# Sums of the second up projection's weights: from VectorE in the projections to adding DMAs in the attention, with two rings of places for the weights

## The chip, the cores and the metric

The kernel runs on one core of a Trainium2 chip. The core has a matrix engine (TensorE, PE in the profile, with its weight loads as PEld), VectorE (DVE), ScalarE (ACT), GpSimd (POOL), a queue engine for DMAs (SP) and 16 DMA engines that all queues share. The metric is the device time of one execution in microseconds (us); a profiled execution lists each instruction, what it waited for and how long.

## What is computed

One layer of a decoder with two parallel token mixers, for 512 positions and a model width of 2048, all in float32. What matters here:

```python
proj = h @ w_in                        # h = RMSNorm(x)
o_a = nsa_attention(q, kv ...) * silu(z_a)
o_b = spatial_gating(uv, ...) * silu(z_b)
merged = g_a * (o_a @ w_up_a) + g_b * (o_b @ w_up_b)
x = x + merged @ w_out
x = x + sigmoid(x @ w_ple_gate) * (p @ w_ple)
return rms_norm(x, final_g)
```

The second up projection is `o_b @ w_up_b`: a 512x1024 by a 1024x2048 product.

## The kernel before

**Precision.** Every float32 matrix is split into a high part (fp32r) and a low part, the rest; a product is three matmuls, high x high, high x low and low x high. ScalarE makes the high part of weights (`high`, line 147), VectorE the low part (`low`, line 153), and TensorE needs both.

**Seven products for eight.** Large products ("S" jobs) take 2x2 blocks by a scheme of Winograd's kind: sums and differences of blocks on both sides, seven products, and sums of the results. The blocks of a weight are b11, b12 (first half of the rows; left and right 512 columns), b21, b22 (second half). The kernel of before uses, for the products named 5, 6, 7 and 4: t5 = b12 - b11, t6 = b22 - t5, t7 = t6 - b11 (made as b22 - b12), t4 = b21 - t6. For most jobs `sum_to` makes them on VectorE (line 271) just before the product. For the two jobs of the second up projection (ub0 and ub1, 1024 columns each) they are made early and kept in DRAM, in `up_sums[i][p]`, and loaded as weights are. The activations of the products have sums of their own (`put_steps`; `ob_dram` holds the parts for ub).

**How the sums are made before.** `up_set(i, k)` (lines 1034 to 1058), for each of the two jobs and four row blocks, has steps: `load` (four 256 KB DMAs on POOL's queue from `w_up_b` into two places `ab` and `cd` of the ring, line 1046), an empty step, `first` and `second`, each with two 128x512 subtractions on VectorE (line 1041) and a 256 KB store behind each on POOL's queue (line 1042), and an empty step. The 40 steps lie in the list `slow`.

**The order of the work.** `gemm()` is a generator that writes out the matmuls of all jobs in order; it yields after every three matmuls, and `fill(n)` takes n such units. At each piece of weights ("sub") it splits the weights of the sub two ahead (`split_to`), which also issues loads on SP's queue where a place has come free (`load_next`), and calls `pop`. `pop` takes a step off `slow` at a rate of 0.85 per call, and steps off `background` at the rate `state["pops"]`. All engines work their own instructions in program order; a wait stops that engine's queue alone. So a DMA on POOL's queue starts when POOL comes to it and what it waits for is there, not when TensorE comes to that place in the program.

**Stages.** Norm and per-layer embedding (0 to about 46 us); the K/V projections: jobs kc, vc, k, then vs (256 columns) and vw (304 columns), until 198 us; beside them `h_chunk` makes the split sums of the activations, with 16 stores of 512 KB on POOL's queue through a tile of three places (h_stage). Then the attention (about 206 to 511 us), in which the jobs q1 to q7 and za0 to za7 (56 subs) are filled in between the attention's own matmuls; POOL has the folds (lines 1285 and 1287), the gating of the compressed branch (1333) and stores of the result (o_d, line 577). `evac_q` asserts that `slow` is empty. Then the jobs u, vn, zb and the merge gates, the first up projection (ua0, ua1), the second (ub0, ub1; about 1130 to 1214 us), the output projection and the end.

**Places of the weights.** `raw` is a tile of three places, 512 KB each; `b12` one of four, for a block that `sum_to` writes into; `add_load` notes the tag and which earlier load must be done with. For ub all loads take `raw`. The activations of ub come back from DRAM by `load_ob(0..6)` on POOL's queue, into places that products of ua1 must have left; `load_gate_b(cg)` loads 1 MB of merge gates for a group of 512 columns, also on POOL's queue, and `gates_a` puts the first gates' multiplications (line 809) into `background`. `final_up` (line 811) closes a product of ub: a multiply on VectorE (line 816) and an addition on POOL (line 817).

Of the kernel before, what the change touches and what calls it, by code (L numbers as in the profile page):

```python
# [13 lines left out]
F32 = mybir.dt.float32  # L14
# [3 lines left out]
ALU = mybir.AluOpType  # L18
# [3 lines left out]
P = 128  # L22
# [42 lines left out]
def kernel(ctx: ExitStack, tc: tile.TileContext, x, p, norm_g, w_in,  # L65
# [108 lines left out]
    def add_load(tag, src, n, cols):  # L174
        r = ring_loads[tag]
        before.append(r[-rings[tag]] if len(r) >= rings[tag] else None)
        r.append(len(loads))
        loads.append((tag, src, n, cols))
        last_sub.append(None)
        return len(loads) - 1  # L180
# [4 lines left out]
    def add_job(job):  # L185
        jobs.append(job)
        if job.kind == "S":
            half, c2 = job.kt // 2, job.c2
            ld = {}
            if job.sums:  # L190
                for p, j in products(job):
                    c, k = {"1": (job.c0, 0), "2": (job.c0, half), "3": (c2, half)}.get(p, (0, 0))
                    src = weights(job, k + 2 * j, 2, c) if p in "123" else job.sums[p][:, 2 * j:2 * j + 2]
                    ld[p, j] = add_load("raw", src, 2, job.cols)
                    last_sub[ld[p, j]] = len(subs)
                    subs.append((job, p, j, ld))
                return
            direct = job.order[0] == "1"
            groups = [[(tag, j) for j in range(half // 2) for tag in tags] for tags in
                      ((("b11",), ("b21",), ("b12",), ("b22",), ("b21'",)) if direct else (("b11", "b12"), ("b22",), ("b21",)))]  # L200
            if direct:
                groups[2].append(groups[1].pop())
            for group in groups:
                for tag, j in group:
                    c, k = (job.c0, c2)[tag[2] == "2"], half * (tag[1] == "2") + 2 * j
                    ld[tag, j] = add_load(tag if tag[1] == "1" else "raw", weights(job, k, 2, c), 2, job.cols)
            for p, j in products(job):
                if not direct:
                    ld["b21'", j] = ld["b21", j]
                last = {"7": ("b11",), "4": ("b12", "b21'"), "3": ("b22",)}.get(p, ())  # L210
                if direct and p == "2":
                    last = ("b21",)
                for tag in last:
                    last_sub[ld[tag, j]] = len(subs)
                subs.append((job, p, j, ld))
            return
        first = 0
        while first < job.kt:
            n = min(job.per_load, job.kt - first)
            li = add_load("raw", weights(job, first, n, job.c0), n, job.cols)  # L220
            for k in range(first, first + n, job.per_sub):
                last_sub[li] = len(subs)
                subs.append((job, k, min(job.per_sub, first + n - k), (li, first)))
            first += n
# [4 lines left out]
    def ring(i, dtype, n=2):  # L229

        return quad["ring"].tile([P, n, S], dtype, tag=f"b11{i}", name="b11")
# [107 lines left out]
    slow = deque()  # L339

    def pop():
        state["late"] += 0.85
        if state["late"] >= 1:
            state["late"] -= 1
            if slow:
                slow.popleft()()
        state["due"] += state["pops"]
        while state["due"] >= 1:
            state["due"] -= 1
            if background:  # L350
                background.popleft()()
# [99 lines left out]
    def finish(name):  # L451
        while name not in done:
            next(run)
        flush()
# [3 lines left out]
    def sub(o, x, y, op=ALU.subtract):  # L458
        x, y = (i.bitcast(F32) if i.dtype == F32R else i for i in (x, y))
        nc.vector.tensor_tensor(out=o, in0=x, in1=y, op=op)  # L460

    def add(o, x, y):
        sub(o, x, y, ALU.add)
# [90 lines left out]

    def evac_q(ft):
        def f(ps):
            assert not slow
            pair = ring((0, 3, 2)[ft % 3], F32R)
            for hh in range(2):
                h = 2 * ft + hh  # L560
                sc = 0.125 / SLOPE[h]
                q = pair[:, hh]
                a = slice(64 * hh, 64 * hh + 64)
                b = slice(64 - 64 * hh, 128 - 64 * hh)
                split(q[a], q[b], ps[a], sc, later=True)
                qs[h] = q
        return f
# [242 lines left out]
                                       op0=ALU.add, op1=ALU.mult)  # L810

    def final_up(i):
        def f(t, c, o, src):
            cg = 2 * i + c // 512
            g, m = (parts_of[n][cg][:, t] for n in "lh")
            nc.vector.scalar_tensor_tensor(out=g, in0=g, scalar=1.0, in1=src, op0=ALU.add, op1=ALU.mult)
            nc.gpsimd.tensor_tensor(out=m, in0=m, in1=g, op=ALU.add)
        return f

    for i in range(2):  # L820
# [210 lines left out]
        split_to(13)  # L1031
    ph_r = ExitStack()
    quad["ring"] = ph_r.enter_context(tc.tile_pool(name="ring", bufs=1))
    ab, cd = (ring(i, F32) for i in range(2))

    def up_set(i, k):

        a, b, c, d = ab[:, 0], ab[:, 1], cd[:, 0], cd[:, 1]

        def minus(o, x, y, p):  # L1040
            nc.vector.tensor_tensor(out=o, in0=x, in1=y, op=ALU.subtract)
            nc.gpsimd.dma_start(up_sums[i][p][:, k], o)

        def load():
            for o, f, col in ((a, k, 0), (b, k, 512), (c, k + 4, 512), (d, k + 4, 0)):
                nc.gpsimd.dma_start(o, w_up_b[f * P:f * P + P, 1024 * i + col:1024 * i + col + 512])

        def first():
            minus(b, b, a, "5")
            minus(c, c, b, "6")  # L1050

        def second():
            minus(a, c, a, "7")
            minus(d, d, c, "4")
        return [load, lambda: None, first, second, lambda: None]

    for i in range(2):
        for k in range(4):
            slow.extend(up_set(i, k))
    mid = ph_ab.enter_context(tc.tile_pool(name="mid", bufs=1))  # L1060
    vt = mid.tile([P, 2, TT, GROUPS, 2 * HD], F32R, name="vt")
    gates = mid.tile([P, TT, 48], F32, name="gates")
# [101 lines left out]
    state["pops"] = 2  # L1164


    ph_b = ph_ab.enter_context(ExitStack())
    att = ph_b.enter_context(tc.tile_pool(name="att", bufs=1))
    tmp_pool.update(p=att, n=1, tag="zt")
# [248 lines left out]
        nc.gpsimd.dma_start(wn[hf], sgu_w[4 * hf:4 * hf + 4].rearrange("g t s -> t g s"))  # L1418
    nc.gpsimd.dma_start(bn, sgu_b)
    finish("za7")  # L1420
    for _ in range(2):
        flush()
    ph_o.close()
# [2 lines left out]
    def new_s4(q, dtype=F32R):  # L1426
        t = s4p.tile([P, 4, S], dtype, tag=f"s4{q}", name=f"s4{q}")
        return t

    def put_steps(w, c, dst, scale):  # L1430

        def put(n, tags, places, sl=slice(0, 512)):

            def f():
                width = sl.stop - sl.start
                h = mix["pool"].tile([P, S], F32R, tag=tags[0], name="pt_" + tags[0], bufs=2 if tags[0] == "v" else 1)
                if len(tags) == 2:
                    l = mix["pool"].tile([P, S], F32R, tag=tags[1], name="pt_" + tags[1])
                else:
                    l = w[n].bitcast(F32R) if width == 512 else h[:, 256:]  # L1440
                high(h[:, :width], w[n][:, sl], scale)

                def rest():
                    low(h[:, :width], l[:, :width], w[n][:, sl], scale)
                    for j, i in enumerate(places):
                        for a, o in enumerate((h, l)):
                            nc.gpsimd.dma_start(dst[:, i, a, c], o[:, 256 * j:256 * j + 256])
                deferred.append(rest)
            return f

        def sums_13():
            f1, f2 = w["1"], w["2"]
            add(f2[:, hi_t], f2[:, hi_t], f1[:, hi_t])
            sub(f1[:, hi_t], f1[:, lo_t], f1[:, hi_t])

        def sums_24():
            f1, f2 = w["1"], w["2"]
            sub(f1[:, lo_t], f2[:, hi_t], f1[:, lo_t])
            sub(f2[:, lo_t], f2[:, lo_t], f1[:, lo_t])
        return put, sums_13, sums_24  # L1460

    def oa_chunk(c):
# [166 lines left out]

    def group_pair(c):  # L1630
        both = {}
        put, sums_13, sums_24 = put_steps(both, c, ob_dram, None)

        def sums_put():
            sums_24()
            put("1", ("g0",), (2, 4))()
        return (group(c, both) + group(c + 4, both) + [nothing, put("2", ("g0", "g1"), (5, 6)), nothing, nothing,
                put("1", ("v",), (0,), lo_t), sums_13, sums_put, nothing, put("2", ("g1",), (3, 1)), nothing])
# [65 lines left out]


    load_ob(5, new_s4(1))
    load_ob(6, new_x(F32R))
    gates_a((2, 3))
    for cg in range(2):
        load_gate_b(cg)  # L1710

    def turn_merged(i, banks, n):

# [240 lines left out]
```

## Time and profile before

| | us |
|---|---|
| median of 3 runs (1562.84 to 1565.43) | 1564.43 |
| the profiled execution | 1564.91 |
| its span | 1562.9 |
| VectorE's waits for loads of w_up_b at line 1041 | 16.6 |
| mean granted clock of TensorE | 0.994 |

The profile's page gives busy time by engine, DMA queues, the chain that ended last and the costliest groups. A row of a wait reads: engine, what it was about to write and its line, the engine or DMA waited for; then us in total, times, longest. A row of a timeline reads: start, length, engine, line, operation, output and inputs, sizes; in brackets the idle time ahead of it and who ended it. Matmuls overlap, so their start-to-start distance tells the rate.

### The profile page before, as it was taken

How to read it: one execution, taken by the hardware profiler on the slowest of the kernel's cores; microseconds unless marked ns; L12 is line 12 of the kernel's file. 1: busy time of each engine (PE TensorE's matmuls, PEld its weight loads, DVE VectorE, ACT ScalarE, POOL GpSimd, SP SyncE). 2: the span in 40 equal slices, each digit the busy share in tenths (PEclk: the TensorE clock that was granted, in tenths of full speed). 3: DMA queues.
4: the chain of work that ended last, by engine and by line, in shares of the span. 5: the costliest groups of instructions: out<-in, count | busy, mean ns of one | idle time of the engine just before them, and what ended most of it. 6: DMA issues, size and time to landing. Idle time of an engine off the chain costs nothing.

```text
span 1562.9 us, 20745 instructions
## 1 busy us (share of the span) xinstructions
PE 1535.5 (98%) x7390; PEld 1283.2 (82%) x7390; DVE 1244.4 (80%) x1933; ACT 805.8 (52%) x1369; POOL 317.8 (20%) x526
## 2 busy tenths in 40 slices
PE   9999899999999999999999999999999999999997
PEld 8888788888888888888888888888877888888886
DVE  6568747898887788978988787787878787878877
ACT  6433336676665555545455444555445343544455
POOL 1323300011022332301222121321123222000100
PEclk9999899999999999999999999999999999999999
DMA  8668852123223985836574746686676478454655
GB/s 320 208 189 267 274 157 68 48 61 102 55 81 122 320 247 175 272 97 208 168 286 108 241 140 221 225 276 242 238 276 221 141 232 266 149 197 167 188 200 191
DMA packets 174311, 298.62 MB, mean 191 GB/s; under 512 B 11752, under 2 KB 89216, under 8 KB 171008
## 3 DMA queue, kind: packets, MB, share of 16 engines
q1 hardware_dynamic: 117456, 157.96, 31.8%
q0 software_dynamic: 56608, 139.07, 26.9%
q8 instruction: 58, 0.95, 0.2%
q14 instruction: 45, 0.37, 0.1%
q10 hardware_dynamic: 144, 0.26, 0.0%
HBM read 227.52 MB, written 69.73 MB: 190 GB/s over the span
## 4 chain that ended last, share of the span: by engine, by line
PE 83%; DVE 5%; DMA 5%; issue 3%; ACT 2%; POOL 1%; DVEq 0%; POOLq 0%; ACTq 0%
PE ps_m L378 6%; PE ps_m L379 6%; PE ps_m L377 6%; PE ps_za L403 2%; PE ps_t L1248 2%; PE ps_za L404 2%; PE ps_za L405 2%; PE ps_wo L416 2%; PE ps_wo L417 2%; PE ps_wo L415 2%; PE ps_pg L378 2%; PE ps_wo L378 2%; PE ps_zb L378 2%; PE ps_vn L379 2%; PE ps_zb L379 2%
## 5 line engine op out<-in xcount | busy, mean ns | idle before, releaser
L147 ACT CAST hs<-b 128x1024 fp32r<-128x1024 f32 x196 | 205.9, 1053 | 226.2 <-PE ps_m L379 66.4
L153 DVE TENSOR_TENSOR ls<-b,hs 128x1024 fp32r<-128x1024 f32 x196 | 239.5, 1223 | 102.1 <-ACT hs L147 100.9
L147 ACT CAST hs<-raw 128x1024 fp32r<-128x1024 f32 x108 | 113.6, 1054 | 130.3 <-PE ps_m L379 28.2
L153 DVE TENSOR_TENSOR ls<-raw,hs 128x1024 fp32r<-128x1024 f32 x108 | 139.2, 1290 | 36.2 <-ACT hs L147 36.1
L153 DVE TENSOR_TENSOR lo<-raw,hi 128x512 fp32r<-128x512 f32 (+1 forms) x184 | 125.6, 688 | 43.6 <-issue 17.0
L147 ACT CAST hi<-raw 128x512 fp32r<-128x512 f32 (+1 forms) x184 | 108.3, 603 | 84.2 <-PE ps_wo L417 19.4
L377 PE MATMUL ps_m<-hs,act_h 128*128 128x512 f32 x256 | 100.5, 393 | 0.0
L378 PE MATMUL ps_m<-ls,act_h 128*128 128x512 f32 x256 | 100.0, 390 | 0.2 <-DVE ls L153 0.2
L379 PE MATMUL ps_m<-hs,act_l 128*128 128x512 f32 x256 | 99.7, 390 | 0.0
L271 DVE TENSOR_TENSOR b<-raw,b 128x1024 f32<-128x1024 f32 x80 | 97.4, 1218 | 1.4 <-DMA raw<-in_w_in_dram 1.0
L271 DVE TENSOR_TENSOR b<-b,b 128x1024 f32<-128x1024 f32 x80 | 97.4, 1218 | 0.0
L147 ACT CAST pth<-ps_t 128x512 fp32r<-128x512 f32 (+1 forms) x88 | 48.0, 545 | 65.8 <-PE ps_t L1248 65.5
L153 DVE TENSOR_TENSOR ptl<-ps_t,pth 128x512 fp32r<-128x512 f32 (+1 forms) x88 | 56.2, 638 | 21.0 <-ACT pth L147 20.0
L1209 ACT ACTIVATE prob<-prob,st 128x512 f32<-128x512 f32 (+3 forms) x128 | 70.7, 556 | 4.0 <-DVE st L1200 3.8
L1200 DVE CUSTOM_DVE_ANT_0 prob<-ps_s,b 128x512 f32<-128x512 f32 (+3 forms) x128 | 56.3, 486 | 10.0 <-PE ps_s L1197 9.7
L378 PEld LDWEIGHTS ps_m<-ls,act_h 128*128 128x128 f32 x256 | 48.1, 188 | 10.6 <-DVE ls L153 1.0
L379 PEld LDWEIGHTS ps_m<-hs,act_l 128*128 128x128 f32 x256 | 48.1, 188 | 10.0
L377 PEld LDWEIGHTS ps_m<-hs,act_h 128*128 128x128 f32 x256 | 48.1, 188 | 9.8
L403 PE MATMUL ps_za<-act_h,hi 128*128 128x512 f32 x128 | 55.7, 436 | 0.0
L403 PE MATMUL ps_q<-act_h,hi 128*128 128x512 f32 x128 | 53.6, 419 | 0.0
L405 PE MATMUL ps_q<-act_h,lo 128*128 128x512 f32 x128 | 50.3, 393 | 1.1 <-DVE lo L153 1.1
L1248 PEld LDWEIGHTS ps_t<-ident,prob 128*128 128x128 f32 x320 | 39.7, 140 | 13.7 <-DVE ptl L153 2.8
(686 smaller groups left out, 4500.4 us busy)
## 6 DMA issues: line engine op xcount, KB each, us to landing
raw<-in_w_in_dram SPq DMA_DIRECT2D x112, 512.0 KB, 4.2
b<-in_w_in_dram SPq DMA_DIRECT2D x56, 512.0 KB, 5.8
raw<-in_w_out_dram SPq DMA_DIRECT2D x24, 512.0 KB, 4.1
raw<-in_w_ple_gate_dram SPq DMA_DIRECT2D x24, 512.0 KB, 3.8
b<-in_w_up_b_dram POOLq DMA_DIRECT2D x32, 256.0 KB, 6.0
t<-b POOLq DMA_DIRECT2D x32, 256.0 KB, 3.7
act_l<-gate POOLq DMA_DIRECT2D x8, 1024.0 KB, 11.7
raw<-t SPq DMA_DIRECT2D x16, 512.0 KB, 4.8
```

The costliest lines, as they stand in the source:

```text
L147: nc.scalar.copy(hi, src)
L153: nc.vector.tensor_tensor(out=lo, in0=src, in1=hi.bitcast(F32), op=ALU.subtract)
L271: nc.vector.tensor_tensor(out=b[o], in0=b[x], in1=b[y], op=ALU.subtract)
L377: nc.tensor.matmul(o, ah, wh, start=st, stop=False, skip_group_check=go)
L378: nc.tensor.matmul(o, ah, wl, start=False, stop=False, skip_group_check=go)
L379: nc.tensor.matmul(o, al, wh, start=False, stop=sp, skip_group_check=go)
L403: nc.tensor.matmul(ps, hi[:, j], ah, start=st, stop=False)
L404: nc.tensor.matmul(ps, hi[:, j], al, start=False, stop=False)
L405: nc.tensor.matmul(ps, lo[:, j], ah, start=False, stop=sp)
L1200: nc.vector.tensor_tensor_reduce(out=pt[:, j * n:j * n + n], in0=o[:, j], in1=b0[:, 512 - n:], scale=-SLOPE[h], scalar=3.0e38, op0=ALU.add ...
L1209: nc.scalar.activation(sl, sl, AF.Exp, bias=st[:, 0, j, hh:hh + 1], scale=-1.0, accum_out=st[:, 1, j, hh:hh + 1])
L1248: nc.tensor.transpose(b[:, (2 * e + hh) * P:(2 * e + hh + 1) * P], pts[hh][:, c:c + P], ident)
```

## The change

The 32 subtractions, 64 DMAs and two places of `up_set` go. In their place 32 DMAs of 512 KB go from DRAM to DRAM on POOL's queue, during the attention: for each sum, job and half of the rows one that copies a block and one that adds a second block to it. Since a DMA adds, all signs are plus: t5 = b12 + b11, t7 = b22 + b12, t6 = t7 + b11, t4 = t6 + b21. This is the scheme before with b12 and b22 negated, so the right 512 columns of each job come out with the other sign and are subtracted in `final_up`, and the sums of the activations get other signs (`negated`). The step rate of `slow` goes from 0.85 to 0.6 per call, and the order is: four copies, four additions, for each of the sums 5, 7, 6, 4. Loads of ub alternate between `raw` and `b12`. Before ub0 the last activation load and two gate loads move, with `fill` between them, and the two gates change order.

```diff
-                    ld[p, j] = add_load("raw", src, 2, job.cols)
+                    ld[p, j] = add_load(("raw", "b12")[len(ld) % 2], src, 2, job.cols)
...
-        state["late"] += 0.85
+        state["late"] += 0.6
...
-            assert not slow
             pair = ring((0, 3, 2)[ft % 3], F32R)
...
-            nc.gpsimd.tensor_tensor(out=m, in0=m, in1=g, op=ALU.add)
+            nc.gpsimd.tensor_tensor(out=m, in0=m, in1=g, op=ALU.subtract if c % 1024 else ALU.add)
...
-    ab, cd = (ring(i, F32) for i in range(2))
-    def up_set(i, k):
-        a, b, c, d = ab[:, 0], ab[:, 1], cd[:, 0], cd[:, 1]
-        def minus(o, x, y, p):
-            nc.vector.tensor_tensor(out=o, in0=x, in1=y, op=ALU.subtract)
-            nc.gpsimd.dma_start(up_sums[i][p][:, k], o)
-        def load():
-            for o, f, col in ((a, k, 0), (b, k, 512), (c, k + 4, 512), (d, k + 4, 0)):
-                nc.gpsimd.dma_start(o, w_up_b[f * P:f * P + P, 1024 * i + col:1024 * i + col + 512])
-        def first():
-            minus(b, b, a, "5")
-            minus(c, c, b, "6")
-        def second():
-            minus(a, c, a, "7")
-            minus(d, d, c, "4")
-        return [load, lambda: None, first, second, lambda: None]
-    for i in range(2):
-        for k in range(4):
-            slow.extend(up_set(i, k))
...
     state["pops"] = 2
+    def up_sum(i, half, p, first, second):
+        ks = slice(2 * half, 2 * half + 2)
+        o = up_sums[i][p][:, ks]
+        def of(name):
+            if name in up_sums[i]:
+                return up_sums[i][name][:, ks]
+            f, c = 512 * (name[1] == "2") + 256 * half, 1024 * i + 512 * (name[2] == "2")
+            return w_up_b[f:f + 256, c:c + 512].rearrange("(k p) c -> p k c", p=P)
+        return [lambda: nc.gpsimd.dma_start(o, of(first)),
+                lambda: nc.gpsimd.dma_start(o, of(second), accum_op=ALU.add)]
+    for p, first, second in (("5", "b12", "b11"), ("7", "b22", "b12"), ("6", "7", "b11"), ("4", "6", "b21")):
+        chains = [up_sum(i, half, p, first, second) for i in range(2) for half in range(2)]
+        for step in range(2):
+            slow.extend(c[step] for c in chains)
+    state["late"] = 0
...
     finish("za7")
+    assert not slow
...
-            add(f2[:, hi_t], f2[:, hi_t], f1[:, hi_t])
+            (sub if negated else add)(f2[:, hi_t], f2[:, hi_t], f1[:, hi_t])
...
-            sub(f1[:, lo_t], f2[:, hi_t], f1[:, lo_t])
-            sub(f2[:, lo_t], f2[:, lo_t], f1[:, lo_t])
+            for o, x in ((f1, f2[:, hi_t]), (f2, f2[:, lo_t])):
+                if negated:
+                    nc.vector.scalar_tensor_tensor(out=o[:, lo_t], in0=x, scalar=-1.0, in1=f1[:, lo_t],
+                                                   op0=ALU.mult, op1=ALU.subtract)
+                else:
+                    sub(o[:, lo_t], x, f1[:, lo_t])
...
-        put, sums_13, sums_24 = put_steps(both, c, ob_dram, None)
+        put, sums_13, sums_24 = put_steps(both, c, ob_dram, None, negated=True)
...
     load_ob(5, new_s4(1))
+    gates_a((2, 3))
+    fill(4)
     load_ob(6, new_x(F32R))
-    gates_a((2, 3))
-    for cg in range(2):
-        load_gate_b(cg)
+    fill(6)
+    load_gate_b(1)
+    fill(8)
+    load_gate_b(0)
```

More of the change, by code (lines that the diff above doesn't have):

```diff
@@ L1428, in new_s4, with put_steps @@
         return t
-    def put_steps(w, c, dst, scale):
+    def put_steps(w, c, dst, scale, negated=False):
         def put(n, tags, places, sl=slice(0, 512)):
```

## The prediction

> **What bounds the kernel now.** First the page's busy times, then the waits of PE, then the stretches in which they fall.
>
> ```profile
> span 1562.9 us, 20745 instructions
> PE 1535.5 (98%) x7390; PEld 1283.2 (82%) x7390; DVE 1244.4 (80%) x1933; ACT 805.8 (52%) x1369; POOL 317.8 (20%) x526
> ...
> PE ps_vw L416 <- DVE lo L153: 6.9, 2, 4.7
> PE ps_ub L378 <- DVE ls L153: 2.3, 4, 1.0
> PE ps_k L405 <- DVE lo L153: 2.1, 1, 2.1
> ...
> PE ps_q L405 <- DVE lo L153: 1.1, 1, 1.1
> PE ps_vw L415 <- DVE vt L153: 0.4, 1, 0.4
> ```
>
> TensorE is the bound: it idles 27.4 us in all (1562.9 - 1535.5), and nothing taken from another engine is worth more than the idle time and the slow clock it causes. 10.5 us of the listed waits lie in the K/V projections and at the first q (ps_k, ps_vw, ps_q), 2.3 us in the second up projection (ps_ub). Both are places that the change touches. The columns of the stretches are length, busy time (instructions) of PE, PEld, DVE, ACT, POOL, then granted clock, DMA share, GB/s.
>
> ```profile
> 131.00:134.00 3.00, 3.00 (x9) 2.33 (x8) 2.73 (x5) 0.73 (x2) 0.00 (x0) 0.52 1.05 391
> 159.00:206.00 47.00, 38.65 (x230) 36.12 (x229) 32.84 (x64) 15.92 (x39) 14.74 (x28) 0.89 0.88 284
> 206.00:511.00 305.00, 303.31 (x1668) 256.13 (x1667) 244.42 (x713) 189.56 (x500) 44.34 (x79) 1.00 0.28 80
> 1130.00:1214.00 84.00, 81.03 (x367) 65.57 (x366) 65.18 (x67) 40.53 (x52) 26.06 (x17) 1.00 0.70 243
> ```
>
> PE loses 8.35 us of the 47 from 159 to 206 by idling, and the DMA engines are 88% busy there. The attention (206 to 511) has only 1.7 us of idle PE and DMA engines that are 28% busy. The second up projection idles 3.0 us.
>
> What makes DVE late is read from VectorE's rows ahead of the two long stalls and from the chain that ended last:
>
> ```profile
> 167.94 0.69 DVE L1041 TENSOR_TENSOR b<-b 128x512 f32<-128x512 f32 x1 [3.56 <-DMA b<-in_w_up_b_dram]
> ...
> 170.47 0.47 DVE L153 TENSOR_TENSOR lo<-raw,hi 128x304 fp32r<-128x304 f32 x1
> ...
> 185.32 0.69 DVE L1041 TENSOR_TENSOR b<-b 128x512 f32<-128x512 f32 x1 [5.15 <-DMA b<-in_w_up_b_dram]
> ...
> 187.03 0.47 DVE L153 TENSOR_TENSOR lo<-raw,hi 128x304 fp32r<-128x304 f32 x1
> ...
> 155.80 5.85 DMA t<-b
> ...
> 163.00 6.17 DMA b<-in_w_up_b_dram
> ```
>
> VectorE works in order. The subtraction of up_set (L1041) stands in front of `lo`, the weights' low part that the matmul wants, and sits waiting for its load; the load was held until the stores of the set before had left the two places (t<-b, then b<-in_w_up_b). This is the loop that the change removes.
>
> **What the early stage loses, by pitch.** A stall costs its wait and the slow clock behind it, so I count starts.
>
> ```profile
> 127.24 0.39 PE L404 MATMUL ps_k<-act_l,hi 128*128 128x512 f32 x1
> 129.77 0.50 PE L405 MATMUL ps_k<-act_h,lo 128*128 128x512 f32 x1 [2.15 <-DVE lo L153]
> ...
> 136.30 0.39 PE L405 MATMUL ps_k<-act_h,lo 128*128 128x512 f32 x1
> ...
> 161.34 0.30 PE L417 MATMUL ps_vw<-hi,act_l 128*128 128x304 f32 x1
> ...
> 168.51 0.30 PE L415 MATMUL ps_vw<-hi,act_h 128*128 128x304 f32 x1
> ...
> L415 PE MATMUL ps_vw<-hi,act_h x64: 296/298/459, 159.6 to 197.4; 128*128 128x304 f32 x64
> L417 PE MATMUL ps_vw<-hi,act_l x64: 296/302/458, 159.8 to 197.6; 128*128 128x304 f32 x64
> ```
>
> Undisturbed 512-column matmuls start 0.227 us apart (six steps in a row around 127); 22 starts from 127.24 to 136.30 should take 5.0 us and took 9.06: 4.1 lost. 304-column ones start 0.138 us apart (52 steps from 161.34 to 168.51); the 191 steps of vw should take 26.4 us and took 38.0: 11.6 lost. The 1.1 us wait at the first q makes it 16.8 us.
>
> The clock: after the 2.15 us wait the granted clock is 0.52 for the next 3 us. The Trainium skill (TensorE: Matmul & The Clock Gate, "What's actually happening") says that the array runs at half clock after an idle window and needs about 3.4 us of work to come back. By that rule each of the three long stalls costs 1.7 us beside its wait; the row agrees with the half clock, and the count by pitch holds this already.
>
> **The change, part by part.**
>
> *Removed: up_set.* 32 subtractions of 0.69 us on VectorE (the rows of L1041 above; 22 us), 64 DMAs of 256 KB that POOL issues at 0.54 us each (35 us of POOL), and 16.8 MB of traffic:
>
> ```profile
> L1046 POOL DMA_DIRECT2D b<-in_w_up_b_dram x32: 537/542/607, 55.1 to 179.7; - x32
> L1042 POOL DMA_DIRECT2D t<-b x32: 540/544/550, 61.9 to 189.0; - x32
> DVE b L1041 <- DMA b<-in_w_up_b_dram: 16.6, 7, 5.2
> 113.30:125.90 12.60, 12.60 (x58) 10.42 (x57) 12.34 (x19) 4.58 (x9) 3.13 (x6) 1.00 0.58 175
> q0 software_dynamic: 7747, 25.55, 47.6%
> ACT h_stage L147 <- DMA hsum<-h_stage: 3.9, 1, 3.9
> hsum<-h_stage POOLq DMA_DIRECT2D x11, 512.0 KB, 6.2
> ```
>
> All 16.6 us of VectorE's waits for these loads go. The stalls at 171 and 187.5 go with them. The one at 129.77 comes from a full VectorE (busy 12.3 of 12.6 us from 113.3 to 125.9), in which four L1041 start 0.6 us apart and take 2.4 us, more than the wait of 2.15. What stays of the 16.8: the 0.6 us at the hand-over of vs to vw (an evacuation), the 1.1 us at q. What is late next is the chain of the split sums (h_chunk): each step sends a 512 KB store that lands in 6.2 us, into three places, and ScalarE has waited 3.9 us for one. With half of POOL's traffic gone I put 1 us on it (between 0 and three such waits, 12). Gain 16.8 - 0.6 - 1.1 - 1.0 = 14.1 us.
>
> *Added: 32 DMAs DRAM to DRAM of 512 KB in the attention, 16 of them adding.* Issue: 32 at 0.54 us is 17 us more on POOL, which is busy 44 of 305 us: hidden. Traffic: POOL's queue moved 25.55 MB from 46 to 200, in 47.6% of the 154 us, so 2.9 us of all DMA engines per MB. 16.8 MB plainly moved is 48 us; with the addends' second read (8.4 MB) 72 us. The DMA share rises from 0.28 to about 0.52. Who could suffer are the weight loads:
>
> ```profile
> DMA to landing us min/median/max: 3.5/3.7/6.4
> ...
> POOL o L1285 <- DVE o L1284: 92.6, 9, 19.2
> ```
>
> There are 30 raw loads in the 290 us, one per 9.7 us, with three places, so a load has ten us and more until its data are used; the worst took 6.4 us to land, and ScalarE waits for none in this stage.
>
> No trace here has an adding DMA. Its nearest row is a plain 512 KB load, 3.7 us; the far bound is the 1 MB gate load, 12.5 us under a full DMA. I take 7.4 us, twice the plain load, since it reads two operands. The added wait: an addition waits on POOL for the copy or sum of its chain, issued four steps earlier. Steps come every 1/0.6 = 1.67 pops; 56 pops in 305 us are 5.4 us each, so a step every 9.1 us and 36 us until the wait. Behind a waiting POOL stand the folds (L1285), the gating of the compressed branch (L1333) and the stores of o32, and behind them SP and PE; but POOL itself waits for VectorE at the folds, 92.6 us in nine waits, so it comes to them early and has that time to give. I take 1 us of cost (0 to 5) for bursts of DMAs that meet a weight load.
>
> The Trainium skill (Collectives: The Full Stack, "The bandwidth ceiling: the fold count and why AG ≠ RS ≠ AR") says that the add in a DMA is free but its two source reads halve the rate. By it the sum stays the one above; no run here has shown it.
>
> *Rings.* The weights of the second up projection now alternate between `raw` (3 places) and `b12` (4 places, idle since the first up projection's last product).
>
> ```profile
> ACT hs L147 <- DMA raw<-t: 18.4, 9, 5.3
> ACT hs L147 <- DMA raw<-in_w_up_b_dram: 10.4, 6, 3.0
> 1123.57 0.37 SPq L243 DMA_DIRECT2D raw<-in_w_up_b_dram  x1
> 1127.90 3.02 SPq L243 DMA_DIRECT2D raw<-t  x2
> 1130.58 9.40 DMA raw<-t
> act_l<-gate POOLq DMA_DIRECT2D x5, 1024.0 KB, 12.5
> ```
>
> The loads are issued in pairs instead of one by one, so the fifth, now issued at 1130.6 and landing after 9.4 us, goes out with the place freed at 1123.6; later leads grow further. That covers ScalarE's 28.8 us of waiting and PE's 3.0 us of idling. Upper bound: each of the four listed waits also costs some 0.2 us of slow restart (the row at 129.77 is 0.50 long instead of 0.39, and the next starts 0.34 on instead of 0.23), 3.8 us; lower bound 0, if the DMA engines and not the places are the limit, or VectorE's contention with POOL's multiply-adds (L817). I take 3.0.
>
> *The rest.* In final_up an addition on POOL becomes a subtraction; eight 128x256 subtractions on VectorE become scalar_tensor_tensor of the same size, in a program whose VectorE is 20% free: nothing. The last load_ob and the two gate loads are issued later in the program and the gates in swapped order. POOL doesn't wait for PE's place in the program, so they still start when the place x is free; gate 1, which is needed first, now lands first: nothing. Rate 0.85 to 0.6: priced above.
>
> *Sum.* 14.1 + 3.0 - 1.0 = 16.1 us. The profiled execution took 1564.9 us (2.0 outside its span), 0.5 above the median 1564.4: 1548.8 against it, 1548.3 against the median. I say 1548.5.
>
> **Rivals.**
> 1. *The early stage is only half repaired*: the h_chunk stores or the full VectorE take up_set's place. For it: ScalarE's 3.9 us wait for hsum. Against it: VectorE's long waits are all for in_w_up_b. Half of 14.1 is lost: 1555.5.
> 2. *Slower: adding DMAs are slow.* The place is POOL's queue in the attention. Eight steps (four copies, four additions) have 73 us, so it decides once a copy and an addition together take over 18 us of DMA time, an addition 14 us at a copy's 3.7, four plain loads. Beyond that POOL falls behind 16 times the excess: at 18 us, 16 x (21.7 - 18.2) = 56 us, less the 17 gained, about 1604. Against it: no transfer in the trace is that slow.
> 3. *No change*: the bursts delay weight loads, each of 16 additions stalling PE by about 1 us: 1564. Against it is the slack above.
>
> **Chances.** Forecast 0.68, with its own range 1543 (all of 16.8 and 3.8, and nothing paid) to 1553; rival 1 0.16; rival 2 0.11; rival 3 0.05. 0.2% (3 us) is about what a measurement of this kernel tells from no change. Faster 0.84, same 0.05, slower 0.11. The range 1543 to 1560 takes in rival 1 and leaves out 2 and 3.
>
> **What would show it.** No DVE L1041; PE's waits at ps_k and ps_vw under 2 us, vw's 191 steps in 27 to 29 us, granted clock 1.00 from 128 to 200; DMA share in the attention near 0.5 and ACT without waits for raw; additions landing in 5 to 12 us; ACT's waits for raw and b12 in ps_ub under 8 us. Wrong, if POOL's waits in the attention are for its own sums, if additions land later than 18 us, or if PE still waits for `lo` in ps_vw.

## The result and the profile after

The changed kernel takes 1542.75 us (median of four runs, 1542.72 to 1543.99) against 1564.2 us before (median of four; the table ahead has the first three). The ratio is 0.9865, with an interval of 0.9848 to 0.9882. That is 21.5 us faster where 16 were forecast, and 0.25 us under the low end of the range.

The page of the changed kernel first, with the head of its list of PE's waits:

```profile
span 1541.9 us, 20629 instructions
...
PE 1527.2 (99%) x7390; PEld 1278.5 (83%) x7390; DVE 1225.7 (79%) x1901; ACT 807.8 (52%) x1369; POOL 312.5 (20%) x494
...
PE ps_spin L965 <- POOL eps_t L87: 1.4, 1, 1.4
PE ps_t L1240 <- DVE ptl L153: 1.3, 1, 1.3
PE ps_pl L411 <- ACT hi L147: 0.6, 1, 0.6
PE ps_ub L378 <- DVE ls L153: 0.4, 1, 0.4
```

TensorE idles 14.7 us instead of 27.4. The waits at ps_k, ps_vw and ps_q are off the list, and ps_ub is down from 2.3 to 0.4 us.

The same reading by stretches, before and then after (length, busy time of PE, PEld, DVE, ACT and POOL, granted clock, DMA share, GB/s). The first two are the K/V projections, 196 to 500 is the attention, and 1114 to 1194 the second up projection:

```profile
46.00:128.00 82.00, 81.44 (x384) 67.36 (x382) 51.43 (x99) 34.13 (x66) 29.02 (x56) 1.00 0.65 204
128.00:200.00 72.00, 62.96 (x416) 60.24 (x417) 55.05 (x95) 23.34 (x49) 22.46 (x42) 0.91 0.88 284
```

```profile
46.00:128.00 82.00, 82.00 (x389) 68.32 (x388) 44.33 (x88) 35.73 (x68) 10.69 (x21) 1.00 0.39 114
128.00:200.00 72.00, 72.00 (x485) 68.07 (x485) 52.84 (x93) 31.16 (x64) 8.64 (x18) 1.00 0.68 204
196.00:500.00 304.00, 302.27 (x1663) 255.04 (x1662) 247.22 (x715) 190.40 (x500) 75.20 (x112) 1.00 0.55 137
1114.00:1194.00 80.00, 79.56 (x368) 65.99 (x367) 66.70 (x69) 40.83 (x52) 26.08 (x17) 1.00 0.66 240
```

From 128 to 200, TensorE goes from 62.96 busy us at clock 0.91 to 72.00 of 72 at clock 1.00, and the DMA share falls from 0.88 to 0.68. The attention pays with DMA time only: share 0.55 instead of 0.28, TensorE still at 1.00.

Where the time went is read from four starts of TensorE: the first product of k (L403), the first of the split sums in u (L377, `hs,act_h`), the first of ub, and the first of the output projection (L415). The rows of a line give the first and the last start. Before, then after:

```profile
L403 PE MATMUL ps_k<-act_h,hi x64: 388/389/628, 81.6 to 135.8; 128*128 128x512 f32 x64
...
L377 PE MATMUL ps_u<-hs,act_h x48: 389/389/500, 518.2 to 584.8; 128*128 128x512 f32 x48
...
L377 PE MATMUL ps_ub<-hs,ob_h x32: 388/389/477, 1130.8 to 1185.1; 128*128 128x512 f32 x32
...
L415 PE MATMUL ps_wo<-hi,act_h x64: 389/389/477, 1215.4 to 1296.2; 128*128 128x512 f32 x64
```

```profile
L403 PE MATMUL ps_k<-act_h,hi x64: 387/389/501, 82.0 to 132.3; 128*128 128x512 f32 x64
...
L415 PE MATMUL ps_vw<-hi,act_h x64: 296/301/304, 156.1 to 182.1; 128*128 128x304 f32 x64
...
L417 PE MATMUL ps_vw<-hi,act_l x64: 302/302/305, 156.3 to 182.4; 128*128 128x304 f32 x64
...
L377 PE MATMUL ps_u<-hs,act_h x48: 389/389/504, 501.7 to 568.4; 128*128 128x512 f32 x48
...
L377 PE MATMUL ps_ub<-hs,ob_h x32: 389/389/476, 1114.4 to 1165.2; 128*128 128x512 f32 x32
...
L415 PE MATMUL ps_wo<-hi,act_h x64: 389/389/476, 1194.9 to 1275.7; 128*128 128x512 f32 x64
```

From k to u: 436.6 before, 419.7 after, 16.9 us gained. From ub to the output projection: 84.6 before, 80.5 after, 4.1 gained. All the rest of the span differs by 0.0 (1041.7 in both). The sum is the 21.0 us by which the spans differ. The 16.9 divide, by the first and last starts of `ps_k` and of `ps_vw` at L415 (before: 159.6 to 197.4), into 3.9 in k, 11.8 in vw and 1.2 between vw and u. vw's 191 steps, by L415 and L417, take 26.3 us instead of 38.0. I call the two distances "early" and "ub" below.

The new DMAs, by the lines that issue them (first the copies, then the additions), each with its time to landing, and POOL's only wait for them:

```profile
L1151 POOL DMA_DIRECT2D t<-in_w_up_b_dram x8: 690/705/743, 187.9 to 302.9; - x8
L1151 POOL DMA_DIRECT2D t<-t x8: 527/547/1047, 348.3 to 440.5; - x8
...
DMA to landing us min/median/max: 4.4/5.4/10.2
...
L1152 POOL DMA_DIRECT2D t<-in_w_up_b_dram x16: 1128/1154/1558, 221.9 to 479.7; - x16
...
DMA to landing us min/median/max: 6.6/7.5/11.7
...
POOL t L1152 <- DMA t<-in_w_up_b_dram: 3.3, 1, 3.3
```

An addition lands in 7.5 us and a copy in 5.4 (medians), well inside the 36 us that the prediction counted from a copy to the addition that waits for it. That distance is a mean: where steps came close together, POOL did wait once, 3.3 us.

### The profile page after: what moved, and what is told of

Its sections match the earlier page's. It is cut to its first block, busy times and chain, and to the rows that moved or that the text cites. A ratio compares the mean times of both kernels' runs of the same rounds, so it can differ in the third digit from the quotient of the medians.

```text
span 1541.9 us, 20629 instructions
## 1 busy us (share of the span) xinstructions
PE 1527.2 (99%) x7390; PEld 1278.5 (83%) x7390; DVE 1225.7 (79%) x1901; ACT 807.8 (52%) x1369; POOL 312.5 (20%) x494
## 3 DMA queue, kind: packets, MB, share of 16 engines
HBM read 235.91 MB, written 78.12 MB: 204 GB/s over the span
## 4 chain that ended last, share of the span: by engine, by line
PE 92%; DVE 4%; ACT 1%; issue 1%; DMA 1%; SPq 0%; POOL 0%; DVEq 0%; ACTq 0%; POOLq 0%
PE ps_m L378 6%; PE ps_m L379 6%; PE ps_m L377 6%; PE ps_za L403 2%; PE ps_t L1240 2%; PE ps_za L404 2%; PE ps_za L405 2%; PE ps_wo L417 2%; PE ps_wo L415 2%; PE ps_wo L416 2%; PE ps_pg L378 2%; PE ps_wo L378 2%; PE ps_pg L377 2%; PE ps_pg L379 2%; PE ps_ua L378 2%; PE ps_zb L379 2%
## 5 line engine op out<-in xcount | busy, mean ns | idle before, releaser
L153 DVE TENSOR_TENSOR ls<-b,hs 128x1024 fp32r<-128x1024 f32 x210 | 262.0, 1248 | 106.5 <-ACT hs L147 104.7
L147 ACT CAST hs<-b 128x1024 fp32r<-128x1024 f32 x210 | 220.7, 1053 | 239.3 <-PE ps_m L379 65.5
L153 DVE TENSOR_TENSOR lo<-raw,hi 128x512 fp32r<-128x512 f32 (+1 forms) x184 | 125.7, 689 | 55.2 <-issue 18.6
L147 ACT CAST hs<-raw 128x1024 fp32r<-128x1024 f32 x94 | 99.0, 1054 | 104.2 <-PE ps_m L379 28.6
L153 DVE TENSOR_TENSOR ls<-raw,hs 128x1024 fp32r<-128x1024 f32 x94 | 116.9, 1244 | 24.3 <-ACT hs L147 24.3
L377 PE MATMUL ps_m<-hs,act_h 128*128 128x512 f32 x256 | 100.5, 393 | 0.0
L378 PEld LDWEIGHTS ps_m<-ls,act_h 128*128 128x128 f32 x256 | 48.1, 188 | 10.7 <-DVE ls L153 1.0
L377 PEld LDWEIGHTS ps_m<-hs,act_h 128*128 128x128 f32 x256 | 48.1, 188 | 9.8
L403 PE MATMUL ps_za<-act_h,hi 128*128 128x512 f32 x128 | 55.8, 436 | 0.0
L403 PE MATMUL ps_q<-act_h,hi 128*128 128x512 f32 x128 | 53.6, 419 | 0.0
L1240 PE MATMUL ps_t<-ident,prob 128*128 128x128 f32 x320 | 49.4, 273 | 1.4 <-DVE ptl L153 1.3
```

Source lines behind the costliest of these rows:

```text
L147: nc.scalar.copy(hi, src)
L153: nc.vector.tensor_tensor(out=lo, in0=src, in1=hi.bitcast(F32), op=ALU.subtract)
L377: nc.tensor.matmul(o, ah, wh, start=st, stop=False, skip_group_check=go)
L378: nc.tensor.matmul(o, ah, wl, start=False, stop=False, skip_group_check=go)
L403: nc.tensor.matmul(ps, hi[:, j], ah, start=st, stop=False)
L1240: nc.tensor.transpose(b[:, (2 * e + hh) * P:(2 * e + hh + 1) * P], pts[hh][:, c:c + P], ident)
```

## The experiments

The theory on trial is the prediction's: in the early stage VectorE's in-order wait for up_set's loads costs the time, and the rings gain their part apart from it. The main rival is that the traffic itself, 64 DMAs in a stage whose DMA engines are 88% busy, costs it. Two distances settle most of it. The table stands ahead of the runs that it sums up; each row is one profiled execution.

```
kernel                          first k   first u   early   lost against after
before                             81.6     518.2   436.6   16.9
after                              82.0     501.7   419.7    0
rings alone                        81.8     516.5   434.7   15.0
move alone                         80.8     500.4   419.6   -0.1
no sums at all                     80.6     500.3   419.7    0
before, more places                82.1     509.5   427.4    7.7
before, loads left out             83.1     509.9   426.8    7.1
before, subtractions left out      81.1     511.1   430.0   10.3
before, traffic only               80.7     520.6   439.9   20.2
after, DMAs moved early            89.2     540.8   451.6   31.9
after, each addition twice         80.9     517.8   436.9   17.2
```

The early stage is the same code in the rows "before" and "rings alone", and they differ by 1.9 us, so a difference of 2 us between two rows says nothing.

**The two halves apart.** First the rings alone, in the kernel before:

```diff
-                    ld[p, j] = add_load("raw", src, 2, job.cols)
+                    ld[p, j] = add_load(("raw", "b12")[len(ld) % 2], src, 2, job.cols)
```

> The kernel before with one edit: the weights of the second up projection alternate between raw and b12. Theory (the three places are the limit there, since each load goes out only when a place comes free): ScalarE's 28.8 us of waiting for these loads falls under 8 us, PE's stalls in ub go, 3.0 to 4.5 us faster than before, 1560 to 1561. Rival (the DMA engines are the limit, 70% busy in that stretch): the waits only move, under 1.5 us gained.

Then the changed kernel with that line put back:

```diff
-                    ld[p, j] = add_load(("raw", "b12")[len(ld) % 2], src, 2, job.cols)
+                    ld[p, j] = add_load("raw", src, 2, job.cols)
```

> The changed kernel with all loads of the second up projection on raw again, so only the move of the sums into the attention is left. Theory (the two gains are separate): the 4 us of the ring come back, 1546 to 1547.5, with the early stage free of stalls. Rival (the gains overlap, because the ring also needs the earlier stage's relief): within 1.5 us of the changed kernel, or the sum of the two single gains misses the whole by over 2 us.

The rings alone took 1560.35 us (ratio 0.9976, 0.9965 to 0.9986), 3.6 us less. The move alone took 1545.34 (0.9880, 0.9865 to 0.9895), 18.6 less. Together 22.2, against 21.5 for both: they add up. What the rings remove is in ScalarE's waits in the second up projection, first with the rings alone and then with the move alone:

```profile
ACT hs L147 <- PE ps_ub L379: 25.7, 17, 1.7
```

```profile
ACT hs L147 <- DMA raw<-t: 16.6, 8, 5.1
ACT hs L147 <- DMA raw<-in_w_up_b_dram: 13.8, 8, 2.9
```

With the rings ScalarE waits for TensorE there and no longer for a load. ub takes 84.6 us before, 84.5 with the move alone and 80.5 with the rings alone.

**VectorE's order, with the traffic kept.** In the kernel before, from the fifth set on, three of the four blocks of the next set are loaded one set ahead; every other set uses columns of o32 that are free then. Traffic, subtractions and pace stay.

```diff
+        other = 4 * i + k in (5, 7)
...
+        def places():
+            if other:
+                return o32[:, 5], o32[:, 6], o32[:, 7], cd[:, 1]
+            return ab[:, 0], ab[:, 1], cd[:, 0], cd[:, 1]
...
+    for n, s in enumerate(sets):
+        ahead = [sets[n + 1][0]] if 4 <= n < 7 else []
+        own = [s[1]] if n > 4 else s[:2]
+        slow.extend([both(*own), both(*ahead), s[2], s[3], none])
```

> The kernel before with more places for up_set from its fifth set on: three of the four blocks of a set are loaded one set ahead into free columns of another tile, the fourth as before. Same subtractions, same traffic, same pace; only the load no longer waits for the store of the set before. Theory (the wait for loads on VectorE is the cost in vw): vw's loss of 11.6 falls to under 5, 1556 to 1559, the stall at 129.77 stays. Rival (the DMA load is the cost): within 3 us of before.

It took 1555.84 us (0.9944, 0.9929 to 0.9959), 9.1 less. A wait, a row of vw and the stretch from 128 to 200:

```profile
DVE b L1045 <- DMA b<-in_w_up_b_dram: 7.0, 4, 4.8
...
L415 PE MATMUL ps_vw<-hi,act_h x64: 296/298/305, 159.3 to 188.7; 128*128 128x304 f32 x64
...
128.00:200.00 72.00, 65.52 (x450) 61.75 (x450) 60.91 (x107) 28.40 (x62) 24.96 (x48) 1.00 0.97 318
```

VectorE's waits for the loads fall from 16.6 to 7.0 us and vw takes 29.4 us between these starts instead of 37.8, while the DMA engines are busier than before (0.97). So some 9 us come from VectorE's waits for these loads and not from the traffic.

The same from the other side: loads only for the first set, so VectorE's waits for them fall to 5.1 us, with all subtractions and stores kept.

```diff
+            if i or k:
+                return
```

> The kernel before with up_set loading only for its first set: the later subtractions run on what lies in the two places, so the sums of the second up projection's weights are left out, and the 32 subtractions and 32 stores stay. Theory (the waits for loads are the cost, not VectorE's work): the two long stalls go, the one at 129.77 (a full VectorE) stays: 11 to 13 us gained, 1551 to 1553. Rival (VectorE's 22 us of work is the cost): under 4 us gained. Rival (DMA load): with half of up_set's traffic gone, about half, 6 to 9 us.

It took 1553.3 us (0.9935, 0.9921 to 0.9948), 10.7 less. vw is whole (26.4 us between these starts, 26.0 in the changed kernel), and what stays is the stall in k and one at the first q:

```profile
L415 PE MATMUL ps_vw<-hi,act_h x64: 296/301/304, 161.0 to 187.4; 128*128 128x304 f32 x64
...
PE ps_k L405 <- DVE lo L153: 2.2, 1, 2.2
...
PE ps_q L405 <- DVE lo L153: 1.4, 1, 1.4
```

**VectorE's work taken away, DMAs kept.** The subtractions go, and each store waits on POOL for the load of its place.

```diff
-            nc.vector.tensor_tensor(out=o, in0=x, in1=y, op=ALU.subtract)
```

> The kernel before without the 32 subtractions of up_set: the loaded blocks are stored as they are, so the sums of the second up projection's weights are left out and all 64 DMAs stay. Theory (VectorE stands in its order at a wait for a load, and `lo` stands behind it): 12 to 16 us of the early stage's 16.8 come back, 1548 to 1552, with the DMA share between 159 and 200 as high as before. Rival (the DMA engines' load makes everything late): the traffic is the same, under 4 us gained.

It took 1555.37 us (0.9945, 0.9932 to 0.9959), only 8.6 less. The stall in k is gone; since it stayed with the loads gone, VectorE's work made it. The rest is not gone: 4.0 us stay lost in vw and 6.4 behind it, around the first q. Other waits stand in VectorE's place (PE's first, then 46 to 225):

```profile
PE ps_q L405 <- DVE lo L153: 3.5, 1, 3.5
...
POOL t L1041 <- DMA b<-in_w_up_b_dram: 32.8, 13, 4.8
...
ACT h_stage L147 <- DMA hsum<-h_stage: 12.1, 4, 4.7
...
ACT hi L147 <- DMA raw<-in_w_in_dram: 6.9, 3, 3.7
```

POOL now stands at its own stores, the stores of the split sums queue behind them, and ScalarE waits for both those and its weights.

**The traffic with nothing waiting on it.** In the kernel before the stores write a constant tile, so neither a subtraction nor a store waits for a load of up_set; all 64 DMAs stay, and the second up projection reads blocks of w_up_b.

```diff
...
-            nc.vector.tensor_tensor(out=o, in0=x, in1=y, op=ALU.subtract)
-            nc.gpsimd.dma_start(up_sums[i][p][:, k], o)
+            nc.gpsimd.dma_start(up_sums[i][p][:, k], b0)
```

> The kernel before with up_set's 64 DMAs and nothing that waits on them: the loads go where they went, the 32 stores write a constant tile to the DRAM tiles of the sums, and the second up projection loads blocks of w_up_b instead, so the sums are left out. In e3_no_vector POOL's queue stood at stores that waited for loads (18.5 us), and the stores of the split sums stood behind. Theory (orders of queues, not bandwidth): with no such wait the early stage loses under 3 us, so 13 us or more are gained, under 1551. Rival (the DMA engines' load by itself delays raw loads and the stores of h_stage): as e3_no_vector, 8 to 10 us gained, 1554 to 1556.

It took 1565.31 us (1.0004, 0.9989 to 1.0019): no gain, against both theories. A wait between 46 and 225, the landing of the raw loads between 46 and 200 (5.5 us in the middle and at most 9.0 before), and the first stretch:

```profile
ACT hi L147 <- DMA raw<-in_w_in_dram: 32.3, 8, 8.8
...
DMA to landing us min/median/max: 3.4/7.2/23.0
...
46.00:128.00 82.00, 74.40 (x337) 61.29 (x336) 34.65 (x72) 27.90 (x55) 25.72 (x50) 0.94 0.58 187
```

With little left to wait for (6.2 us in all, for the load before in the same place), POOL issued the 32 DMAs of the first four sets within 29 us (55 to 84); in the kernel before they are spread over 68 us (55 to 123). The DMA share from 55 to 84 is 1.02, against 0.75 before, SP's weight loads land as late as 23 us, and TensorE then idles 6.0 of the 44 us from 84 to 128. The waits had cost time, and they had also spread the traffic out.

**The change's own DMAs, put where up_set was.** The changed kernel with the 32 DMAs DRAM to DRAM in the K/V projections, at 0.68 steps per call:

```diff
-        state["late"] += 0.6
+        state["late"] += 0.68
```

(the block with `up_sum` and its loop stands where up_set's stood)

> The changed kernel with its 32 DMAs in the old stage: the same copies and additions are taken off the list in the K/V projections, at 0.68 per call, where up_set was; the attention has none. It parts where the work is from who does it. Theory of the prediction (VectorE in its order was the cost): VectorE has no part in it, so under 3 us of the gain is lost, 1543 to 1546. Rival (after e3_no_vector and e6_traffic_only: that stage's DMA engines can't take this traffic without making raw loads and the stores of the split sums late): 8 us or more are lost, 1550 to 1560.

It took 1571.48 us (1.0039, 1.0025 to 1.0053), 28.7 more than the changed kernel and 0.4% slower than before; the rival had the direction, and neither range took it in. The profiled execution is the longest of its six (1583.12, 11.6 over their median), and its first k is already 7.2 us late, so its row of the table tells where the time goes and not how much. Its waits, its raw loads and the first stretch, as above:

```profile
ACT hi L147 <- DMA raw<-in_w_in_dram: 58.9, 11, 10.8
...
DMA to landing us min/median/max: 3.4/9.9/30.9
...
46.00:128.00 82.00, 70.11 (x304) 56.62 (x303) 30.26 (x66) 25.05 (x50) 22.62 (x33) 0.90 0.69 174
```

POOL, no longer held by VectorE, issued 15 of the 32 DMAs between 55 and 89, and the DMA share from 55 to 84 is 1.06. So the adding DMA as such gains nothing; in this stage, issued like this, it loses more than up_set did. The gain is the place. Whether the same DMAs held to an even pace would fit into the K/V projections was not tried.

**The attention without them, and at another pace.** The DMAs left out, ub's weights read from blocks of w_up_b:

```diff
...
-            slow.extend(c[step] for c in chains)
+            pass
```

> The changed kernel without its 32 DMAs in the attention: the sums are left out, and the second up projection loads blocks of w_up_b in their place. Theory (the attention hides them whole): within 1 us of the changed kernel, 1542 to 1543.5. Rival (bursts meet weight loads, the 1 us of the prediction or more): 1 to 3 us faster than the changed kernel, 1540 to 1541.5.

1543.97 us (0.9873, 0.9857 to 0.9890), not faster than with them. The attention:

```profile
196.00:500.00 304.00, 302.27 (x1663) 255.12 (x1662) 246.99 (x714) 189.82 (x500) 46.38 (x81) 1.00 0.28 85
```

TensorE is busy 302.27 us at a DMA share of 0.28, and was 302.27 at 0.55, and "early" is 419.7 in both: the attention hides the DMAs whole. Issuing them faster:

```diff
-        state["late"] += 0.6
+        state["late"] += 1.0
```

> The changed kernel with the steps taken at 1.0 per call in place of 0.6, so the 32 DMAs lie in the first 32 of the attention's 56 calls. Theory (even pace matters little there, the loads have ten us to spare): within 1 us of the changed kernel. Rival (bursts meet weight loads or the folds): 2 to 6 us slower.

1542.88 us (0.9860, 0.9845 to 0.9875): this faster pace doesn't matter there. Nor does the order of the last loads before ub0:

```diff
-    gates_a((2, 3))
-    fill(4)
     load_ob(6, new_x(F32R))
-    fill(6)
-    load_gate_b(1)
-    fill(8)
-    load_gate_b(0)
+    gates_a((2, 3))
+    for cg in range(2):
+        load_gate_b(cg)
```

> The changed kernel with the last activation load, gates_a and the two gate loads ahead of the second up projection in the old order and place. Theory (POOL starts them when the place is free, whatever their place in the program): within 1 us of the changed kernel, 1542 to 1543.7. Rival (the order is part of the gain in ub, as gate 1 is needed first): 1.5 to 3 us slower than the changed kernel.

1542.87 us (0.9866, 0.9851 to 0.9881).

**How much room the attention has.** Each addition done two or three times in a row, each waiting for the one before:

```diff
-        return [lambda: nc.gpsimd.dma_start(o, of(first)),
-                lambda: nc.gpsimd.dma_start(o, of(second), accum_op=ALU.add)]
+        def adds():
+            for n in range(2):
+                nc.gpsimd.dma_start(o, of(second), accum_op=ALU.add)
+        return [lambda: nc.gpsimd.dma_start(o, of(first)), adds]
```

> The changed kernel with each addition made twice in a row on the same destination, so the sums hold the second block twice. The second waits for the first: about 15 us of POOL's queue per step. By the formula of the prediction, which gave 1670 for x_adds3 (measured 1665): 3.7 + 15 - 18.2 = 0.5, times 16, 8 us: 1551. Rival (the slack is used up only as a whole: 16 waits of 7.5 are 120 us, and POOL had over 200 us of waiting to give): within 2 us of the changed kernel, 1543 to 1545.

> The changed kernel with each addition made three times in a row on the same destination, so the sums hold the second block three times. Each waits for the one before: about 3 x 7.5 = 22 us of POOL's queue per step, by the measured landing time. By the formula of the prediction (POOL falls behind 16 times what a copy and an addition take over 18.2 us): 3.7 + 22.5 - 18.2 = 8 us, times 16, about 1670. Rival (POOL had over 200 us of waiting in the attention to give, so only what doesn't fit is paid): 16 x (3 x 1.15 + 15) + 20 = 315 us of work and waits against some 230 free, up to 85 us slower, 1545 to 1630.

Twice took 1562.51 us (0.9984, 0.9974 to 0.9995), three times 1665.41 (1.0650, 1.0628 to 1.0671). The waits of the first, with ScalarE's from 480 to 520:

```profile
POOL t L1153 <- DMA t<-in_w_up_b_dram: 124.5, 16, 11.2
...
ACT zt L587 <- POOL o L1279: 14.0, 1, 14.0
...
PE ps_u L377 <- ACT hi L147: 10.2, 1, 10.2
```

Of the 17.2 us lost, 12.9 fall in the first 48 matmuls of u (23.7 us from 494.1 to 517.8, 10.8 in the changed kernel). POOL runs late through the attention at a cost of only 4.3 us up to there, and most of the bill comes at the hand-over to u: ScalarE waits 14.0 us for the last fold (L1279), and TensorE waits 10.2 us for the weights (`hi`) that ScalarE makes behind that. With three additions POOL waits 215.1 us and is still issuing at 605.

## Why the prediction was right, and where its sum was off

- *What bounds, and the loop.* Right. The waits at ps_k, ps_vw and ps_q went, the clock is 1.00 from 128 to 200, vw takes 26.3 us (27 to 29 was said). The count by pitch held in its parts: 4.1 in k, 11.6 in vw and 1.1 at q were said, and 3.9, 11.8 and 1.2 came back. That VectorE's in-order wait carried vw's loss is shown with the traffic kept (vw at 29.4 us instead of 37.8) and with the loads gone (26.4). That the stall in k came from a full VectorE is shown by its going with the subtractions and staying with the loads gone.
- *14.1 in the early stage* was the term most mis-sized: 16.9 by the distance. The step that failed was to take 0.6 us for the hand-over to vw, 1.1 at q and 1.0 for the stores of the split sums as losses that the change leaves; none of the three came. The wait at the hand-over (0.4 us) is missing already with the rings alone, whose early stage is unchanged. The stall at q is there in every run that keeps DMAs for these sums in the K/V projections, with the subtractions (0.9 to 1.4 us) or without (3.5 to 8.1), and in no run that has none there; which of them feed it isn't shown. The stores land in 4.3 us (median, 46 to 200) instead of 6.2 and raw loads in 3.6 instead of 5.5, and ScalarE waits for neither.
- *3.0 for the rings.* Measured 4.1 by the distance and 3.6 by the run of the rings alone; the upper bound was 3.8. All of ScalarE's 28.8 us of waits for loads went, by the mechanism named: SP's issues go out in pairs.
- *-1.0 for the attention.* Measured 0.0. The terms under it: DMA share 0.55 (0.52 said), landing 7.5 us (7.4 said), a copy 5.4 (3.7 taken). That the landing was met is luck: it was twice 3.7, and it came as 1.4 times 5.4. POOL's issue was undersized: 16 at 1.15, 8 at 0.70 and 8 at 0.55 are 28.4 us, not 17. The cover named, POOL's waits for VectorE at the folds, was large enough: 133.3 us of them are left.
- *Sign edits, order of the loads, rate: nothing.* The order was tried alone, and of the rate a faster one: both within 0.2 us. The sign edits weren't tried alone; ub with the rings takes 80.5 us with and without them.
- *The range.* Its low end was the case of all 16.8 and 3.8 gained and nothing paid. That case came, with 0.1 and 0.3 us more. Of the 4.9 us between the 16.1 forecast and the 21.0 of the spans, 2.8 are the early stage, 1.1 the rings and 1.0 the attention: in each the sum was more cautious than it had to be.
- *Rival 1* (half repaired) fell for this change, yet it is what happens where the waits go and the traffic stays: 10.3 and 20.2 us stay lost. The prediction had the loop right, and took it for the whole; it didn't see that the loop also paced the DMAs.
- *Rival 2* (slow additions) fell: they land in 7.5 us, and the copy and the addition take 12.9 together, under its 18.2. Its price formula, with its copy of 3.7, gave 1670 us for three additions (1665 measured), but 1551 for two (1562.5 measured); with the measured copy of 5.4 it gives 1698 and 1578, so the first agreement is partly luck. With two, most of the loss is paid at the end, where one fold waits for whatever stands in POOL's queue; the formula has no such term.
- *Rival 3* (bursts delay weight loads) fell in the attention, and is what the same DMAs do in the K/V projections.

Open: how the 16.9 us divide between order, VectorE's work and traffic. The single removals overlap (9.2, 9.8 and 6.6 us gained by the table), and no run removes one of them wholly with the others unchanged. Subtractions on VectorE during the attention were not tried, nor were the new DMAs in the K/V projections at an even pace.

## What to carry to other kernels

A wait in an in-order queue can be two things, a delay and a brake on the traffic behind it, so before taking it away ask what the freed queue will issue at once and whose loads it meets. Side work belongs in the stage where DMA engines are idle and the weight loads have lead (here a DMA share of 0.28 and one load per 9.7 us; in the K/V projections of the changed kernel one per 5.1), and leaving the work out of that stage is a cheap run that tells what it costs there. Measure the distance between two starts of the bounding engine: it told apart gains that the waits' list mixes.

## What the runs showed of the hardware

- An adding DMA of 512 KB DRAM to DRAM holds POOL 1.15 us at its issue, against 0.70 for a copy from the weights' rows and 0.55 for one between two packed buffers, and lands in 7.5 us (6.6 to 11.7) against 5.4. That is 1.4 times the copy. The Trainium skill (Collectives: The Full Stack, "The bandwidth ceiling: the fold count and why AG ≠ RS ≠ AR") says of the ring steps of a ReduceScatter that two source reads halve the rate. No run here has such a ring; a single adding DMA of 512 KB took 1.4 times a copy's landing time and not twice.
- The profile counts 235.91 MB read from HBM after and 227.52 before, 8.4 more, and 8.4 more written. Copies and additions read 16.8 MB from their sources where up_set read 8.4, so a second read of 8.4 MB, that of the additions' destinations, doesn't appear in that count.
- Weight loads on SP's queue landed as late as 30.9 us when POOL had issued its DMAs in a burst (DMA share 1.06 from 55 to 84), against 9.0 at most before (0.75) and 7.1 after. The Trainium skill (DMA: Bandwidth & Descriptors, "Issuing engines are not separate DMA queues") says that DMAs from all engines run interleaved on the same 16; the trace agrees.
- 32 DMAs raised the DMA share by 0.27 over 304 us, 82 us of all engines (72 were estimated), without a measurable loss on TensorE (302.27 us busy with them and without).
